# A hybrid decoder layer on one core: both products of a recurrence pair ahead of their copies, attention values in 32-column quarters beside page sets, and longer planner leads

## The chip, the cores and the metric

The kernel runs on one core of a Trainium2 chip. TensorE (PE) multiplies and transposes into PSUM banks; VectorE (DVE), ScalarE (ACT) and GpSimd (POOL) work on SBUF and, DVE and ACT, on PSUM; the queues of SyncE (SP), ACT and POOL start the transfers. The metric is the device time of one launch, in microseconds (us).

## What is computed

One layer for 512 prompt tokens and 8 sequences of 4 sample tokens (TOK = 544 columns). Two branches run in parallel: MoBA attention (block-sparse, over 2048 cached rows of each sample sequence) and an HGRN2 recurrence. They are merged by gates, and a convolutional FFN follows. The recurrence of the reference, cut:

```python
def step(S, xs):
    qc, kc, gc, vc = xs
    b = jnp.cumsum(gc, axis=2)
    diff = jnp.where(tri[...], b[:, :, :, None, :] - b[:, :, None, :, :], -jnp.inf)
    A = jnp.einsum('bhtd,bhsd,bhtsd->bhts', qc, kc, jnp.exp(diff))
    o = jnp.einsum('bhts,bhsv->bhtv', A, vc) + jnp.einsum('bhtd,bhdv->bhtv', qc * jnp.exp(b), S)
    S_new = jnp.exp(b_last)[..., None] * S + jnp.einsum('bhsd,bhsv->bhdv', kc * jnp.exp(b_last - b), vc)
    return S_new, o
...
o_b = rmsnorm(o_b, hg_norm_g) * silu(hg)
y_a = jnp.dot(o_a, w_a_out)
y_b = jnp.dot(o_b, w_b_out)
mixed = sigmoid(ga) * y_a + sigmoid(gb) * y_b
x = x + g1 * jnp.dot(mixed, w_o)
```

## The kernel before

All activations are feature-major: 128 features on the partitions, 544 token columns in two halves of 272. Each large product is split into three of reduced type (`hi*xh + hi*xl + lo*xh`, L123 by way of `gemm_chunk` and `pieces`); ACT makes `whi` and DVE makes `wlo` of each weight tile (L195, L198). Such a product, out `g`, is called a gemm row here. The layer runs in stages: the first projections (to 55 us of the span), then a woven stage, then `w_b`, `w_o`, the FFN.

In the woven stage PE's order is written by a planner at build time. `Paced` keeps a planned time `pe.t` that grows with each product, by 0.095 more when the shape of the array (rows, columns) changes. The main chain is the list of jobs `ORDER` and `LAST` (projections) and then the eight `w_a` jobs. Beside it run `Side` generators: each `yield` names a lead, the planned time after which it wants PE again, and whether it is `tiled` (its products use 32 or 64 of 128 columns). `serve` is asked between gemm chunks (12 gemm rows): it runs the earliest due side; a lone tiled one waits up to `SLACK` for company. When the jobs run out, `finish_sides` runs the remaining sides with nothing between them. The other engines' orders are set by the scheduler, which may run their work early.

The sides are: `moba` (32 page sets: 16 of scores, `ms<-pg`, then 16 of values, `macc<-pg`), `attention` (four head pairs m by four query blocks q: scores, softmax on DVE and ACT, transposes of `K` into `s` banks, values `acc<-eb,vtm`), `recur` (four heads j by eight levels of `LEVELS + (0,)`, taken in four pairs), `ada_rest` (the rest of the modulation, 16 transfers `wadl`, ending in a transpose of `smr`), and `recur_sample` (states of the sample sequences `in_S`, then norms of the outputs `ob`, four statistics `s<-EX,con`).

Of one head's recurrence: `level_ready` makes the operands `EX` of a level; `level_mm` multiplies them, and for the levels from 16 down DVE then copies the wanted entries by mask into `Ab` and `As` (L991, L994). `rec_turn` and `rec_state` make the states, `rec_gather` and `rec_out` the output `ob`. PSUM has eight banks: `g` (3, rotating), `s` (2, rotating), `ms`, `acc`, `macc`.

After the fourth statistic, ACT takes logarithm and exponential of the scales `rr`; DVE multiplies `ob` by `rr` (L198) and by gate and gain (L1232), ACT rounds `obh`, DVE makes `obl`; then the `w_b` products (`g<-obh`) start.

## Time and profile before

| | |
|---|---|
| time before, median of 3 runs | 1011.13 us (1010.74 to 1011.80) |
| the profiled execution's own time | 1011.28 us |
| its span, first to last instruction | 1009.6 us |
| PE busy | 958.6 us, 95% of the span |
| DVE, ACT, POOL busy | 579.6, 474.2, 104.7 us |
| woven stage, in the span | about 55 to 517 us |

PE's busy time counts matmuls that overlap, with modelled ends, so that the distance from one start to the next says more than the duration of one. An idle time with a releaser behind an arrow tells which engine's instruction ended last before the work could go on.

### The profile page before, as it was taken

Reading aid. Unit: us, or ns where it says so; the run is one execution under the profiler, and the core shown is the slowest. Engines: PE = TensorE matmul, PEld = TensorE weight load, DVE = VectorE, ACT = ScalarE, POOL = GpSimd, SP = SyncE. Lnnn points to the kernel's source line nnn. Section 1 sums busy time; section 2 is a strip of 40 time slices with the busy share of each in tenths; the row PEclk is TensorE's granted clock in tenths of the full one; section 3 lists DMA queues with packets and bytes.
Section 4 is the critical chain, followed back from the end, with each engine's and each line's share of the span. In section 5 each row is a group of like instructions: output and inputs, shape, how many; then the busy total and the mean of one; then the engine's idle time right before and its main releaser. Section 6 shows DMA issues by size and latency. Waiting matters only on the chain.

```text
span 1009.6 us, 23648 instructions
## 1 busy us (share of the span) xinstructions
PE 958.6 (95%) x8759; PEld 874.3 (87%) x8759; DVE 579.6 (57%) x1479; ACT 474.2 (47%) x938; POOL 104.7 (10%) x162
## 2 busy tenths in 40 slices
PE   5899999999999989999999999999999999999994
PEld 3898887776778878868998999999999999999994
DVE  4654646644767766435657767655555555555553
ACT  3354565636454633313624556544444444555552
POOL 1212212212210000000013220000000000011111
PEclk9899999999999999999999999999999999999997
DMA  9799999889893555562225514322222223566662
GB/s 313 272 352 345 338 324 319 301 301 317 298 328 139 215 181 171 175 243 94 76 82 200 168 43 138 124 84 93 86 84 93 86 94 93 156 177 170 205 179 71
DMA packets 95894, 190.05 MB, mean 188 GB/s; under 512 B 10657, under 2 KB 26146, under 8 KB 93730
## 3 DMA queue, kind: packets, MB, share of 16 engines
q1 hardware_dynamic: 82722, 141.03, 42.2%
q0 software_dynamic: 8160, 26.75, 7.4%
q10 hardware_dynamic: 4896, 20.76, 5.7%
q8 instruction: 69, 1.13, 0.4%
q14 instruction: 47, 0.39, 0.1%
HBM read 181.47 MB, written 7.02 MB: 187 GB/s over the span
## 4 chain that ended last, share of the span: by engine, by line
PE 82%; DVE 6%; ACT 4%; DMA 3%; issue 2%; POOL 1%; SPq 1%; DVEq 0%; ACTq 0%; POOLq 0%
PE g L123 67%; PE macc L123 4%; PE ms L123 4%; PE s L123 3%; PE acc L123 2%; DMA s<-in_S 1%; PE g L127 1%; PE s L127 1%; DVE wlo L198 1%; ACT whi L195 1%; DMA wadl<-in_w_adl 1%; POOL tgb L1244 1%; DMA xt<-in_x 1%; DMA wraw<-in_w_o 1%; SPq L355 0%
## 5 line engine op out<-in xcount | busy, mean ns | idle before, releaser
L198 DVE TENSOR_TENSOR wlo<-wraw,whi 128x512 fp32r<-128x512 f32 (+1 forms) x300 | 202.4, 676 | 212.0 <-ACT whi L195 208.1
L195 ACT ACTIVATE whi<-wraw 128x512 fp32r<-128x512 f32 (+1 forms) x300 | 185.5, 619 | 274.4 <-PE g L123 256.0
L123 PE MATMUL g<-hh,whi 128*128 128x272 f32 x712 | 213.8, 301 | 2.0 <-ACT hh L195 1.4
L123 PE MATMUL g<-hh,wlo 128*128 128x272 f32 x712 | 206.6, 290 | 0.6 <-DVE wlo L484 0.5
L123 PE MATMUL g<-hl,whi 128*128 128x272 f32 x712 | 206.5, 290 | 0.4 <-DVE hl L1246 0.4
L123 PE MATMUL g<-h2h,whi 128*128 128x272 f32 x704 | 202.4, 289 | 0.0
L123 PE MATMUL g<-h2l,whi 128*128 128x272 f32 x704 | 201.4, 288 | 0.0
L123 PE MATMUL g<-h2h,wlo 128*128 128x272 f32 x704 | 198.9, 288 | 0.0
L123 PEld LDWEIGHTS g<-hh,whi 128*128 128x128 f32 x712 | 135.3, 190 | 17.9 <-issue 11.4
L123 PEld LDWEIGHTS g<-hl,whi 128*128 128x128 f32 x712 | 135.3, 190 | 1.1 <-DVE hl L1246 0.6
L123 PEld LDWEIGHTS g<-hh,wlo 128*128 128x128 f32 x712 | 135.0, 190 | 1.1 <-DVE wlo L484 0.8
L123 PEld LDWEIGHTS g<-h2l,whi 128*128 128x128 f32 x704 | 132.5, 188 | 0.1
L123 PEld LDWEIGHTS g<-h2h,whi 128*128 128x128 f32 x704 | 132.3, 188 | 0.2
L123 PEld LDWEIGHTS g<-h2h,wlo 128*128 128x128 f32 x704 | 130.9, 188 | 0.0
L123 PE MATMUL g<-ah,wlo 128*128 128x272 f32 x352 | 101.4, 288 | 1.2 <-DVE wlo L198 1.2
L123 PE MATMUL g<-ah,whi 128*128 128x272 f32 x352 | 101.8, 289 | 0.0
L123 PE MATMUL g<-al,whi 128*128 128x272 f32 x352 | 101.6, 288 | 0.0
L123 PEld LDWEIGHTS g<-ah,wlo 128*128 128x128 f32 x352 | 66.1, 188 | 1.5 <-DVE wlo L198 1.4
L123 PEld LDWEIGHTS g<-ah,whi 128*128 128x128 f32 x352 | 66.3, 188 | 0.1
L123 PEld LDWEIGHTS g<-al,whi 128*128 128x128 f32 x352 | 66.2, 188 | 0.1
L1286 POOL TENSOR_TENSOR sq<-sq,sq 128x272 f32<-128x272 f32 x24 | 21.3, 886 | 384.8 <-ACT sq L1277 384.7
L1380 DVE SCALAR_TENSOR_TENSOR cv<-U,sv,cv 128x560 f32<-128x560 f32 x44 | 35.3, 802 | 16.5 <-ACT cv L1378 15.7
(317 smaller groups left out, 1484.9 us busy)
## 6 DMA issues: line engine op xcount, KB each, us to landing
wraw<-in_w_up SPq DMA_DIRECT2D x98, 256.0 KB, 2.5
wraw<-in_w_in SPq DMA_DIRECT2D x82, 256.0 KB, 4.5
wraw<-in_w_down SPq DMA_DIRECT2D x80, 256.0 KB, 2.8
pg<-in_K SPq DMA_DIRECT2D x77, 256.0 KB, 6.3
pg<-in_V SPq DMA_DIRECT2D x77, 256.0 KB, 6.3
wadl<-in_w_adl ACTq DMA_DIRECT2D x16, 1024.0 KB, 5.3
pg<-in_K POOLq DMA_DIRECT2D x51, 256.0 KB, 5.9
pg<-in_V POOLq DMA_DIRECT2D x51, 256.0 KB, 6.2
```

The source lines that it names most:

```text
L123: return self.eng.matmul(out, lhsT, rhs, **kw)
L127: return self.eng.transpose(out, in_, ident)
L195: return act.activation(out, in_, AF.Copy, scale=scale)
L198: return dve.tensor_tensor(out, a, b, op=op)
L1244: pool.tensor_tensor(tgb[:, m], tga[:, m], tgb[:, m], op=OP.add)
L1286: pool.tensor_tensor(sqa[f], sqa[f], s, op=OP.add)
L1380: dve.scalar_tensor_tensor(a, U[:, t:t + W], cw[:, t, j:j + 1], a, op0=OP.mult, op1=OP.add)
```

## The change

Seven things change, all in the woven stage.

1. Pairs of levels: `level_mm` loses its copies, which become `level_keep`; `recur` calls both products and then both copies. A result tile `pb` holds two levels and not three, so that each pair has a bank of its own; `big` moves from an `s` bank to `ms`; `rec_turn` and `rec_state` move from `g` banks to `s` banks.
2. Level 64 is computed as 8 products of 32 columns for 4 of 64.
3. Attention values are computed as four products of 32 columns where there were two of 64, and each group is a side of its own (`aside`, tiled, slack 8.0), which is dropped in beside a page set, or run by `values()` before the next transposes at the latest.
4. `pot` and `vst` are padded with zeros to 128 rows (memsets on POOL).
5. Leads: `LV` 6.0 to 7.0, attention's scores to transposes 3.0 to 4.0 (plus 0.8 q), `rec_out` 3.5 to 6.5, `moba_own` 0 to 4.0, the first value set of the second group 0 to 3.0, `smr` 1.5 to 4.0, statistics 2.0 and 1.2 to 3.5 and 1.5.
6. `recur_sample` loads the first two states earlier, waits 5.0 before the transpose of `vi`, and 4.0 where it waited 8.0 for the first pair of states.
7. `Side` has a slack of its own.

```diff
@@ -49,7 +49,7 @@
 WR, WS = 4, 3
-SLACK, LT, SETS, LV, ADA = 2.5, 3.0, 7.2, 6.0, 3.6
+SLACK, LT, SETS, LV, ADA = 2.5, 3.0, 7.2, 7.0, 3.6
 ORDER = "k0 v0 k1 k2 k3 v1 v2 v3 f0 q0 i0 f1 q1 i1 f2 q2 i2 f3 q3 i3 a0 a1 a2 a3 a4 a5 a6 a7 g0 g1 g2 g3"
@@ -131,8 +131,8 @@
-    def __init__(self, gen, due=0.0, tiled=False):
-        self.gen, self.due, self.tiled = gen, due, tiled
+    def __init__(self, gen, due=0.0, tiled=False, slack=None):
+        self.gen, self.due, self.tiled, self.slack = gen, due, tiled, SLACK if slack is None else slack
@@ -276,7 +276,7 @@
                 run(flat[0])
-            elif due and (len(due) > 1 or pe.t - due[0].due > SLACK or pe.mode[1] < 128):
+            elif due and (len(due) > 1 or pe.t - due[0].due > due[0].slack or pe.mode[1] < 128):
                 run(due[0])
@@ -510,7 +510,8 @@
     ks = pM.tile([128, 4, 32], F32, name="ks")
-    vst = pM.tile([32, 512], F32, name="vst")
+    vst = pM.tile([128, 512], F32, name="vst")
+    pool.memset(vst, 0.0)
     qT, kT, vtm, vts, halfway = {}, {}, {}, {}, {}
@@ -654,8 +655,9 @@
         pe.transpose(tb[:32, :128], po_, ident)
-        pot = pM.tile([32, 128], F32, name="pot", tag="pot", bufs=2)
-        dve.tensor_copy(pot, tb[:32, :128])
+        pot = pM.tile([128, 128], F32, name="pot", tag="pot", bufs=2)
+        pool.memset(pot, 0.0)
+        dve.tensor_copy(pot[:32], tb[:32, :128])
         d["rl"], d["pot"] = l9[:, 9:10], pot
@@ -678,10 +680,11 @@
             yield 1.0
+        yield 4.0
         tb = gbank()
             pe.transpose(tb[:32, 128 * m:128 * m + 128], vs[:, m], ident)
-        dve.tensor_copy(vst, tb[:32, :])
+        dve.tensor_copy(vst[:32], tb[:32, :])
@@ -717,6 +720,8 @@
                         yield 1.0
+                    if what is moba_values and g and not j:
+                        yield 3.0, True
                     what(g, j)
@@ -780,9 +785,9 @@
         for j in range(q + 1):
-            for h2 in (1, 0):
-                pe.matmul(acc[64 * h2:64 * h2 + 64, 128 * q:128 * q + 128], vtm[m][:, 128 * j + 64 * h2:128 * j + 64 * h2 + 64],
-                          pTs[h2][:, 128 * j:128 * j + 128], start=j == 0, stop=j == q, skip_group_check=True)
+            for y in (3, 2, 1, 0):
+                pe.matmul(acc[32 * y:32 * y + 32, 128 * q:128 * q + 128], vtm[m][:, 128 * j + 32 * y:128 * j + 32 * y + 32],
+                          pTs[y // 2][:, 128 * j:128 * j + 128], start=j == 0, stop=j == q, skip_group_check=True)
         if q == 3:
@@ -790,33 +795,41 @@
     def attention():
-        past, parts = None, {}
+        parts, past = {}, []
+
+        def values():
+            if past:
+                attend_values(*past.pop())
+
+        def aside():
+            values()
+            return
+            yield
+
         for m in range(4):
...
                 parts[m] = attend_split(m)
-                if past:
-                    yield 2.0, True
-                    attend_values(*past)
-                    past = None
                 yield 5.0
             acc = None
+            if m:
+                yield 2.0
             for q in range(4):
                 ps_ = attend_scores(q, *parts[m])
-                if past:
-                    attend_values(*past)
                 if q == 3 and m + 1 in qT and m + 1 in kT:
                     parts[m + 1] = attend_split(m + 1)
-                yield 3.0 + 0.8 * q
+                yield 4.0 + 0.8 * q
+                values()
                 acc = acc or abank()
...
                     yield 1.0
-                past = (m, q, acc, pTs)
+                past.append((m, q, acc, pTs))
+                sides.append(Side(aside(), pe.t + 1.8 + 0.3 * q, True, 8.0))
                 yield 1.8 + 0.3 * q
         yield 0.5, True
-        attend_values(*past)
+        values()
@@ -911,7 +924,7 @@
     def rec_turn(j, k2):
-        tb = gbank()
+        tb = sbank()
         for c in range(4):
@@ -922,7 +935,7 @@
             return
-        tb = gbank()
+        tb = sbank()
         for c in range(4):
@@ -961,11 +974,12 @@
         if h == 64:
-            big[j] = sbank()
+            big[j] = msbank()
             for c in range(4):
-                a = col(c)
-                pe.matmul(big[j][0:64, 64 * c:64 * c + 64], L[:, a:a + 64], R[:, a + 64:a + 128],
-                          start=True, stop=True, skip_group_check=True)
+                for y in range(2):
+                    a = col(c) + 32 * y
+                    pe.matmul(big[j][32 * y:32 * y + 32, 64 * c:64 * c + 64], L[:, a:a + 32], R[:, col(c) + 64:col(c) + 128],
+                              start=True, stop=True, skip_group_check=True)
             return
@@ -975,22 +989,28 @@
         bi = li - 2
-        if bi % 3 == 0:
+        if bi % 2 == 0:
             pb[j] = sbank()
-        z = 128 * (bi % 3)
+        z = 128 * (bi % 2)
         for c in range(4):
...
         r = slice(32 * j, 32 * j + 32)
-        zs = 384 + 32 * (bi % 3)
+        zs = 256 + 32 * (bi % 2)
         if h <= 2:
                       skip_group_check=True)
+
+    def level_keep(j, li):
+        if li < 2:
+            return
+        bi, r = li - 2, slice(32 * j, 32 * j + 32)
+        z, zs = 128 * (bi % 2), 256 + 32 * (bi % 2)
         dve.copy_predicated(Ab[j], base[:, bi, None, :].to_broadcast([128, 4, 32]),
                             pb[j][:, z:z + 128].rearrange("p (c t) -> p c t", c=4))
-        if h <= 2:
+        if bi > 2:
             dve.copy_predicated(As[r], base[r, bi, :], pb[j][r, zs:zs + 32])
@@ -1001,7 +1021,7 @@
                             big[j][64 * y:64 * y + 32, 256:384].rearrange("p (c t) -> p c t", c=4))
-        later(3.5, lambda: rec_out(j))
+        later(6.5, lambda: rec_out(j))
@@ -1043,6 +1063,8 @@
             level_mm(j, li + 1)
+            level_keep(j, li)
+            level_keep(j, li + 1)
             if li + 2 == n:
@@ -1063,7 +1085,7 @@
         dve.tensor_copy(sm, pa)
-        yield 1.5
+        yield 4.0
         pt = gbank()
@@ -1133,10 +1155,20 @@
+    s0s = {}
+
+    def s0_load(p):
+        s0s.clear()
+        for j in (p, p + 1):
+            s0s[j] = pT_.tile([128, 2 * TOK], F32, name="s0", tag="s0", bufs=2)[:, :1024].rearrange("p (b d) -> p b d", b=8)
+            sync.dma_start(s0s[j], i["S0"][j])
+
     def recur_sample():
...
             yield 1.0
+        s0_load(0)
+        yield 5.0
         tb = gbank()
@@ -1156,14 +1188,14 @@
         for p in range(0, G_H, 2):
-            s0s, rvs = {}, {}
+            rvs = {}
+            if p:
+                s0_load(p)
             for j in (p, p + 1):
...
                    bsel[:96, :, None].to_broadcast([96, NB, 128]), OP.mult)
-                s0s[j] = pT_.tile([128, 2 * TOK], F32, name="s0", tag="s0", bufs=2)[:, :1024].rearrange("p (b d) -> p b d", b=8)
-                sync.dma_start(s0s[j], i["S0"][j])
-            yield 8.0, True
+            yield (8.0 if p else 4.0), True
             for g in range(2):
@@ -1198,7 +1230,7 @@
             sq_ = act.activation(sq, ob[j], AF.Square)
-            yield (2.0 if j == 0 else 1.2)
+            yield (3.5 if j == 0 else 1.5)
             for f in range(2):
```

How the order of PE and DVE moves, at three places. The first is PE at the last pair of head 0 (levels 1 and 0; operands `EX`, and `Q`, `K`). Before:

```order
L123 MATMUL g<-hl,whi 128x272
L123 MATMUL g<-hh,wlo 128x272
L123 MATMUL s<-EX 32x32 [waits DVE_49,Activation_49]
L123 MATMUL s<-EX 32x32 x16
L123 MATMUL s<-Q,K 32x32 [waits DVE_49]
L123 MATMUL s<-Q,K 32x32 x16
```

and after the change:

```order
L123 MATMUL macc<-vst,pot 32x512 x3
L123 MATMUL s<-EX 32x32 [waits DVE_49,Activation_49]
L123 MATMUL s<-EX 32x32 x16
L123 MATMUL s<-Q,K 32x32 x17
L123 MATMUL g<-hh,whi 128x272
L123 MATMUL g<-hl,whi 128x272
```

The second product has lost its wait for DVE. The second place is PE around the last statistic (`s<-EX,con`), ahead of the `w_b` products. Before:

```order
L123 MATMUL g<-hl,whi 128x272
L123 MATMUL g<-hh,wlo 128x272
L123 MATMUL s<-EX,con 128x272 x2
L123 MATMUL g<-hh,whi 128x272
L123 MATMUL g<-hl,whi 128x272
```

and after:

```order
L123 MATMUL g<-oal,whi 128x272
L123 MATMUL g<-oah,wlo 128x272
L123 MATMUL s<-EX,con 128x272 x6
L123 MATMUL g<-obh,whi 128x272 x3
L123 MATMUL g<-obl,whi 128x272
L123 MATMUL g<-obh,wlo 128x272
```

Before, 72 gemm rows of gate jobs and the 192 of `w_a` (`oah`, `oal`) stand between the last statistic and the first `g<-obh`; now none does, and the last three statistics stand together. The third place is DVE, from the last scales `rr<-s` to the last `obl`. Before:

```order
L1205 TENSOR_SCALAR rr<-s 128x272 [waits PE_49]
L198 TENSOR_TENSOR wlo<-wraw,whi 128x512 [waits DMAHW6_49,Activation_49]
L1232 SCALAR_TENSOR_TENSOR ob<-ob,hg_8871,G_7469 128x544 [waits DVE_49]
L1232 SCALAR_TENSOR_TENSOR ob<-ob,hg_8871,G_7618 128x544 [waits DVE_49]
L198 TENSOR_TENSOR wlo<-wraw,whi 128x512 [waits DMAHW7_49,PE_49,Activation_49]
L198 TENSOR_TENSOR ob<-ob,rr 128x544 [waits Activation_49]
L198 TENSOR_TENSOR ob<-ob,rr 128x544 [waits DVE_49]
L198 TENSOR_TENSOR obl<-ob,obh 128x544 [waits Activation_49]
L1232 SCALAR_TENSOR_TENSOR ob<-ob,hg_8871,G_7736 128x544 [waits DVE_49]
L198 TENSOR_TENSOR obl<-ob,obh 128x544 [waits Activation_49]
```

and after:

```order
L1237 TENSOR_SCALAR rr<-s 128x272 [waits PE_49] x3
L198 TENSOR_TENSOR ob<-ob,rr 128x544 [waits DVE_49,Activation_49]
L198 TENSOR_TENSOR ob<-ob,rr 128x544 [waits DVE_49]
L1264 SCALAR_TENSOR_TENSOR ob<-ob,hg_8974,G_7226 128x544 [waits DVE_49]
L1264 SCALAR_TENSOR_TENSOR ob<-ob,hg_8974,G_7480 128x544 [waits DVE_49]
L198 TENSOR_TENSOR ob<-ob,rr 128x544 [waits Activation_49]
L198 TENSOR_TENSOR ob<-ob,rr 128x544
L198 TENSOR_TENSOR obl<-ob,obh 128x544 [waits Activation_49]
L1264 SCALAR_TENSOR_TENSOR ob<-ob,hg_8974,G_7956 128x544 [waits DVE_49]
L198 TENSOR_TENSOR obl<-ob,obh 128x544 [waits Activation_49]
L1264 SCALAR_TENSOR_TENSOR ob<-ob,hg_8974,G_8078 128x544 [waits DVE_49]
L198 TENSOR_TENSOR obl<-ob,obh 128x544 [waits Activation_49] x2
```

All twelve operations on `ob` and `obl` (4 by `rr`, 4 by gate, 4 remainders) now stand behind the last scale, with no split of weights among them.

## Rows read from the trace of the kernel before

**Rows 1.** The page: busy time, share of the span, instructions of each engine.
```profile
PE 958.6 (95%) x8759; PEld 874.3 (87%) x8759; DVE 579.6 (57%) x1479; ACT 474.2 (47%) x938; POOL 104.7 (10%) x162
```

**Rows 2.** PE's waits: total us, times, longest us.
```profile
PE acc L123 <- DMA s<-in_S: 2.0, 1, 2.0
PE g L127 <- DVE smr L1065: 1.8, 1, 1.8
...
PE macc L123 <- DVE S L702: 1.7, 1, 1.7
...
PE g L127 <- DVE vi L848: 1.4, 1, 1.4
```

**Rows 3.** Groups by form: x count | busy us, mean ns | idle before, releasers.
```profile
L123 PE MATMUL acc<-eb,vtm 128*64 128x128 f32 x160 | 12.3, 283 | 0.0
L127 PE MATMUL s<-con,K 128*128 128x128 f32 x80 | 12.0, 275 | 3.2 <-DVE K L766 1.4 <-ACT F L195 0.9 <-ACT whi L195 0.5
L123 PE MATMUL s<-EX 128*32 128x32 f32 x720 | 11.5, 198 | 6.2 <-DVE Ab L991 5.6 <-ACT F L195 0.5
...
L123 PE MATMUL s<-Q,K 128*32 128x32 f32 x136 | 2.0, 199 | 2.3 <-DVE As L994 2.3
```

**Rows 4.** Timeline, PE, at a pair: start, us, line op, count [idle before <-releaser].
```profile
276.24 0.29 PE L123 MATMUL g<-hh,wlo 128*128 128x272 f32 x1
276.46 0.46 PE L123 MATMUL s<-EX 128*32 128x32 f32 x32
277.44 0.46 PE L123 MATMUL s<-EX 128*32 128x32 f32 x32 [0.52 <-ACT F L195]
```

**Rows 5.** Timeline, PE: a group of attention values and the page set behind it.
```profile
120.43 1.09 PE L123 MATMUL acc<-eb,vtm 128*64 128x128 f32 x16
121.45 1.93 PE L123 MATMUL ms<-pg,qbd 128*32 128x256 f32 x32
```

**Rows 6.** Timeline, PE: four transposes into one quarter of the columns.
```profile
154.82 0.61 PE L127 MATMUL g<-con,vs 128*32 128x128 f32 x4
```

**Rows 7.** Timeline, PE: the second pair of sample states, waiting for its load.
```profile
451.57 0.62 PE L123 MATMUL acc<-s,QEs 128*32 128x512 f32 x1 [1.97 <-DMA s<-in_S]
...
454.89 0.43 PE L123 MATMUL g<-hh,whi 128*128 128x272 f32 x1
455.12 0.43 PE L123 MATMUL g<-hl,whi 128*128 128x272 f32 x1
```

**Rows 8.** Stretches: us, busy (count) of PE, PEld, DVE, ACT, POOL; PEclk, DMA share, GB/s.
```profile
600.00:900.00 300.00, 300.00 (x2394) 299.87 (x2393) 171.77 (x453) 152.71 (x276) 4.63 (x5) 1.00 0.34 108
452.90:456.30 3.40, 3.40 (x11) 2.24 (x10) 1.60 (x7) 0.00 (x0) 0.00 (x0) 0.50 0.01 3
```

**Rows 9.** Timeline, PE: the last statistic, and the first product of `w_b`.
```profile
482.39 1.08 PE L123 MATMUL s<-EX,con 128*128 128x272 f32 x4
...
517.11 0.29 PE L123 MATMUL g<-obh,whi 128*128 128x272 f32 x1
```

**Rows 10.** Timeline, ACT, behind the last square: table load, logarithm.
```profile
478.72 0.66 ACT L1200 ACTIVATE EX<-ob 128x544 f32<-128x544 f32 x1 [0.18 <-PE s L123]
479.39 1.28 ACT L1207 ACT_TABLE_LOAD   x1
480.69 1.11 ACT L1209 ACTIVATE rr<-rr 128x1088 f32<-128x1088 f32 x1
```

**Rows 11.** Timeline, DVE: scales, gates and last remainder of the outputs.
```profile
483.40 1.35 DVE L198 TENSOR_TENSOR ob<-ob,rr 128x544 f32<-128x544 f32 x2
...
485.62 1.48 DVE L1232 SCALAR_TENSOR_TENSOR ob<-ob,hg,G 128x544 f32<-128x544 f32 x2
...
497.24 0.72 DVE L198 TENSOR_TENSOR obl<-ob,obh 128x544 fp32r<-128x544 f32 x1
```

**Rows 12.** Timeline, DVE and PE: the last operand of another pair, and that pair.
```profile
351.45 0.42 DVE L198 TENSOR_TENSOR EX<-EX,Q 128x256 f32<-128x256 f32 x1
...
353.08 0.48 PE L123 MATMUL s<-EX 128*32 128x32 f32 x32
```

## Prediction

> **What bounds the kernel now.** I read the page first: PE is busy 95% of the span and the next engine 57% [rows 1], so the question is where PE stands still or works for nothing, and not how fast the others are. The list of PE's waits comes next [rows 2], then idle time by kind of product [rows 3], then the timeline at the places that both name. All the waits that this change can reach lie in the woven stage. Outside it PE is dense: 2394 products in 300 us of the FFN, 0.1253 us each, at the full granted clock [rows 8]. I use 0.125 for a gemm row below.
>
> **Part by part: the pairs of levels.** In a pair PE runs the 16 or 17 products of one level, waits until DVE has copied them, and runs the next level [rows 4]. There are 16 pairs; four are levels 64 and 32, which have no copy between them, so 12 pauses remain. The idle time named by form is 6.2 + 2.3 = 8.5 us [rows 3]. It counts from the modelled end of the last product; products start about 0.01 us apart when nothing holds them (32 rows in 0.46, one row alone lasting 0.198 [rows 3, 4]), so each pause also costs the 0.19 us in which a row drains: 12 x 0.19 = 2.3. Together 10.8. The pair shown bears it out: 0.98 us from start to start, of which 16 products need 0.26. After the change the second product stands ahead of both copies, in a bank that only its own pair uses, and nothing is late next as long as its operand is there. The closest case of the 12 is a pair that began at 353.08 with its last operand finished at 351.87 [rows 12], 1.2 us earlier, and the lead to it grows. I take -10.3, between -5.5 (half the pauses return as waits for operands) and -10.8.
>
> **Changes of array width.** From a gemm row to a 32-column product the step is 0.22 us where 0.125 is usual [rows 4]; a switch costs 0.095. Walking through both orders product by product I count 144 switches before and 122 after: quarters share the width of the page sets, level 64 that of level 32, and the padded `vst` and `pot` that of their set. 22 x 0.095 = -2.1.
>
> **Quarters.** A step is two products (4 rows) on two halves of the array; the 40 steps are 160 rows [rows 3]. Four steps (16 rows) take 1.02 us to the next set [rows 5], so a step 0.23 with the switch. In four strips the same 128 columns pass side by side: 0 us, if the four run together as the four of a page set do (32 rows of 256 columns in 1.93 us [rows 5]: 0.06 a row, although one alone would take twice the 0.11 that 128 columns need). If they ran one after another, as four transposes into one strip do (0.11 apart, (0.61 - 0.28) / 3 [rows 6]), a step would take 8 x 0.11 = 0.88, and 40 steps +26. I take 0, since the page set is nearest.
>
> Of the Trainium skill, TensorE: Matmul & The Clock Gate, section "Wait — 56ns, not 53.3ns?", speaks against doubling the count of products: it gives a floor of about 25 ns between starts, and some 62 ns per matmul with hardware decoding off. By 62 ns a step of 8 rows would take 0.5 and the 40 steps +11 us. The level products do not show either floor: 32 rows lie in 0.46 us, so that the trace disagrees and I leave it at 0.
>
> **Other waits that leads reach.** The transpose of `vi` (1.4), of `smr` (1.8), the first value set of the second group (1.7), and the load of the second pair of states (2.0 [rows 2]). The last one is larger in fact: to the 1.97 idle comes the drain of the row before, 0.6, the time that one of this form lasts [rows 7], so 2.55; and the granted clock then was 0.50 for 3.4 us, the lower of its levels, 1.2 GHz [rows 8], with rows 0.23 apart [rows 7], which cost about 1.5 more. Leads grow by 2.5 to 5 us at each, and the loads of `wadl` that shared the queues with `in_S` now lie earlier. Bounds: 0 and 1.6 + 2.0 + 1.75 + 2.55 + 1.5 = 9.4 (each wait with its drain). I take -8.9. Transposes of `K` idle 3.2, 4.1 with the drains [rows 3]; the lead grows by 1 us, but the distance in products at q = 3, where most of it falls, hardly grows: -2.0, bounds 0 and -4.1. Against that, in the changed order one group of values (second head pair, q = 1) stands directly behind its transposes, and PE must wait for two ACT copies: +1.0, bounds 0 and +1.5. The two memsets of `pot` stand early in POOL's order, ahead of the page loads that could hold them, so nobody waits for them: 0.
>
> **The cover ahead of `w_b`.** This is the price. Before, the last statistic starts at 482.39 and the first `w_b` product at 517.11 [rows 9]; between them lie 264 gemm rows, 33 us, under which ACT and DVE finish `ob`. Longer leads push the recurrence and its tail back while the jobs run on; in the changed order none of these rows is left and the last three statistics stand together. So the chain is bare. With t = 0 at the second statistic's start (0.9 us each): its end frees a square buffer, the last square ends at 1.8 (0.66), table load 1.28, then logarithm, exponential, logarithm, exponential of 1.11 each [rows 10]: first exponential at 5.35, second at 7.6. DVE starts at 5.4 and has twelve operations, 0.68 for a scale, 0.74 for a gate, 0.72 for a remainder [rows 11]: four until 8.3, the other eight until 14.0. PE has finished the statistics at 3.3, 0.6 later than dense since each waits for a bank. Until 14.1 it finds 27 rows whose operands are ready (3.4 us; three groups are interleaved). Idle: 14.1 - 3.3 - 3.4 + 0.6 = 8.0. After a pause of this kind the clock fell before [rows 7, 8], so I add 2.0 (the 1.5 us seen there, to 3.0 if it lasts twice as long). Together +10.0, bounds +5 and +13. What hid this was gemm rows; nothing else can.
>
> **Sum.** -10.3 - 2.1 - 8.9 - 2.0 + 1.0 + 10.0 + 1.0 (small new waits that a new order brings; bounds -1 and +4) = -11.3. The profiled execution took 1011.28, 1.7 more than its span; the median is 1011.13, so the two agree. 1011.28 - 11.3 = 1000.0.
>
> **Rivals.** *The tail is hidden after all*: if scales and gates go by quicker, or the rows between fill the hole, it costs 2 for 10: 992.0. For it: the scheduler spread three groups into it. Against: the twelve DVE operations alone last 8.6 us. Chance 0.09.
>
> *Waits move and do not go*: the pairs wait for the second operand instead of the copy, and leads are eaten because the planner's time and real time part. Half the gains (23.3 / 2) remain against +12: 1011.6, within 0.2% of the time before. For it: the margin of only 1.2 us [rows 12]. Against: that pair's lead grows, and it is the closest. Chance 0.10.
>
> *The clock stays low behind the hole* (slower side): PE comes out of the hole with scattered rows, and if the clock then stays at 1.2 GHz through the 192 rows of `w_b`, each costs 0.23 - 0.125 = 0.10 more, +20 for the 2 in the sum: 1018. It decides from some 133 rows on ((11.3 + 2) / 0.10). For it: the hole is longer than the wait at 449 us. Against: there the clock was back after 3.4 us of work. Chance 0.04.
>
> *Quarters run one after another* (slower too): +26, 1026. Against it are the page sets. Chance 0.02.
>
> **How the numbers follow.** My forecast, 1000.0, has 0.75: with the ends that I hold plausible it reaches from 993 to 1007. The range takes in part of the two nearest rivals: 992 to 1009. 0.2% is 2.0 us and about what a measurement of this kernel can tell from no change, so faster means under 1009.1: forecast and hidden tail, with a third of the moved waits, 0.87; same 0.06; slower 0.07.
>
> **What would show it.** Right: in the changed profile the waits on `Ab` and `As` are gone from PE's list; the waits on `vi`, `smr`, `in_S` and `S` are gone; a new one stands at the first `obh` and `obl`, 6 to 10 us in sum, around 495 us, with the granted clock at half just behind it; value groups show 32 columns and the same 0.2 us per step. Wrong: PE waits inside pairs for `EX`; or the hole is under 4 us; or PE waits for pages, whose transfers share queues that carry more per us when PE is faster.

## The result and the profile after

The changed kernel takes 999.43 us (median of 4 runs, 998.9 to 1001.82) against 1010.93 (median of 4 runs of the kernel before beside them): a ratio of 0.9894, 95% interval 0.9872 to 0.9916. That is 11.5 us faster; the prediction said 11.3 and 1000.0 us. The profiled execution took 999.2 us; its span is 997.5, 12.1 less than before, and the times read from traces below are of these two spans.

The page of the changed kernel, busy time of each engine, answers to [rows 1]:

```profile
PE 954.1 (96%) x8951; PEld 875.8 (88%) x8951; DVE 577.5 (58%) x1479; ACT 474.4 (48%) x939; POOL 104.4 (10%) x165
```

PE has 192 products more (160 of values, 32 of level 64) and is busy 4.5 us less. Its list of waits (total us, times, longest us) answers to [rows 2]:

```profile
PE g L123 <- ACT obh L195: 4.1, 1, 4.1
PE s L127 <- DVE K L771: 2.4, 4, 0.9
...
PE g L123 <- ACT tga L1100: 1.3, 1, 1.3
...
PE g L123 <- DVE obl L198: 0.9, 1, 0.9
PE macc L123 <- DMA wadl<-in_w_adl: 0.8, 1, 0.8
...
PE acc L123 <- ACT eb L195: 0.6, 1, 0.6
```

The four waits of [rows 2] (`in_S`, `smr`, `S`, `vi`) are gone, and no wait on `Ab` or `As` is left. New are the first `obh` and `obl` of `w_b`, a bank of a gate job that ACT empties late (`tga`), one transfer `wadl` and the values directly behind their transposes (`eb`). The groups by form answer to [rows 3]:

```profile
L127 PE MATMUL s<-con,K 128*128 128x128 f32 x80 | 12.3, 277 | 3.0 <-DVE K L771 2.4 <-ACT K L769 0.3
...
L123 PE MATMUL acc<-eb,vtm 128*32 128x128 f32 x320 | 12.0, 276 | 0.6 <-ACT eb L195 0.6
L123 PE MATMUL s<-EX 128*32 128x32 f32 x656 | 8.5, 198 | 0.0
...
L123 PE MATMUL s<-Q,K 128*32 128x32 f32 x136 | 2.2, 198 | 0.0
```

Idle time before the levels fell from 6.2 + 2.3 to 0, that before the transposes of `K` hardly (3.2 to 3.0). A pair in PE's timeline, which answers to [rows 4]:

```profile
287.25 0.76 PE L123 MATMUL s<-EX 128*32 128x32 f32 x64
287.84 1.50 PE L123 MATMUL macc<-pg,pT 128*32 128x512 f32 x12
```

Both levels (64 rows) now go by in 0.59 us, where the pair shown before needed 1.27. The price stands at the end of the woven stage, PE's timeline from the last statistics on (it answers to [rows 9]):

```profile
491.89 1.08 PE L123 MATMUL s<-EX,con 128*128 128x272 f32 x4
493.14 0.70 PE L123 MATMUL s<-EX,con 128*128 128x272 f32 x2 [0.17 <-DVE rr L1237]
493.99 1.99 PE L123 MATMUL s<-EX,con 128*128 128x272 f32 x6 [0.16 <-DVE rr L1237]
500.12 1.05 PE L123 MATMUL g<-obh,whi 128*128 128x272 f32 x3 [4.14 <-ACT obh L195]
502.03 0.59 PE L123 MATMUL g<-obl,whi 128*128 128x272 f32 x1 [0.87 <-DVE obl L198]
```

Between them lies the chain that the prediction laid out: on ACT and DVE the last exponential, the first product with the scales and the last remainders (they answer to [rows 10] and [rows 11]):

```profile
498.32 1.11 ACT L1243 ACTIVATE rr<-rr 128x1088 f32<-128x1088 f32 x1
```

```profile
497.32 1.36 DVE L198 TENSOR_TENSOR ob<-ob,rr 128x544 f32<-128x544 f32 x2 [0.86 <-ACT rr L1243]
...
503.92 1.53 DVE L198 TENSOR_TENSOR obl<-ob,obh 128x544 fp32r<-128x544 f32 x2
```

Two stretches of that place (busy time and count of PE, PEld, DVE, ACT, POOL; granted clock, DMA share, GB/s) answer to [rows 8]:

```profile
497.80:508.10 10.30, 7.11 (x30) 6.80 (x31) 7.56 (x12) 4.21 (x6) 0.00 (x0) 0.50 0.00 0
508.10:528.70 20.60, 20.57 (x164) 20.35 (x164) 17.30 (x26) 7.83 (x13) 10.62 (x7) 1.00 0.42 131
```

The granted clock fell to 0.50 (1.2 GHz) while PE stood idle and came back at 508.1. To see where the 12.1 us lie, I added up for each kind of product the time from its start to the start of the next one, from 60 us to the first product of `w_b`:

| | before | after | |
|---|---|---|---|
| products of levels | 23.1 | 11.7 | -11.4 |
| sample states (`s,QEs`, `rv,k2x`) | 9.7 | 5.7 | -4.0 |
| attention values | 12.9 | 9.9 | -3.0 |
| statistics, to the first `w_b` product | 2.9 | 8.9 | +6.1 |
| all PE products | 457.1 | 440.1 | -17.0 |

Of the values' 3.0, some 1.75 is the wait on `S`, which before the change stood behind the last group of values; the rest is the change of width, below. `w_b` itself then takes 28.5 us from first to last product where it took 24.0, which gives 4.5 back; behind it the two kernels differ by 0.3 us.

### The profile page after: what moved, and what is told of

It is laid out like the page before. It is cut to its first block, busy times and chain, and to the rows that moved or that the text cites. A ratio compares the mean times of both kernels' runs of the same rounds, so it can differ in the third digit from the quotient of the medians.

```text
span 997.5 us, 24024 instructions
## 1 busy us (share of the span) xinstructions
PE 954.1 (96%) x8951; PEld 875.8 (88%) x8951; DVE 577.5 (58%) x1479; ACT 474.4 (48%) x939; POOL 104.4 (10%) x165
## 4 chain that ended last, share of the span: by engine, by line
PE 85%; DVE 5%; ACT 4%; DMA 2%; issue 2%; SPq 1%; POOL 0%; DVEq 0%; ACTq 0%; POOLq 0%
PE g L123 70%; PE macc L123 4%; PE ms L123 4%; PE s L123 3%; PE acc L123 2%; PE s L127 1%; PE g L127 1%; DVE wlo L198 1%; DMA wadl<-in_w_adl 1%; DMA xt<-in_x 1%; DMA wraw<-in_w_o 1%; SPq L355 0%; ACT hh L398 0%; DVE hsr L198 0%; ACT tga L650 0%
## 5 line engine op out<-in xcount | busy, mean ns | idle before, releaser
L1412 DVE SCALAR_TENSOR_TENSOR cv<-U,sv,cv 128x560 f32<-128x560 f32 x44 | 35.3, 802 | 16.5 <-ACT cv L1410 15.8
```

The costliest lines, as they stand in the source:

```text
L1412: dve.scalar_tensor_tensor(a, U[:, t:t + W], cw[:, t, j:j + 1], a, op0=OP.mult, op1=OP.add)
```

## Experiments

The question was not whether the sum was right but whether its terms were. Each run is compared with the changed kernel (999.4) or the kernel before (medians of 1010.3 to 1011.3 in the several sets of runs).

### The pairs alone

In the kernel before, only the first edit is made: both products, then both copies, each pair's result in a bank of its own.

```diff
             level_mm(j, li)
             level_mm(j, li + 1)
+            level_keep(j, li)
+            level_keep(j, li + 1)
```

> The kernel before with the first edit alone: both products of a pair ahead of their copies, each pair's result in a bank of its own, and level 64 in the ms bank; the leads, the values in halves and the order of PE's products are those of before, and the 264 gemm rows of cover ahead of w_b stay. Theory (the pairs are worth what the prediction gave, 10.3 us): the waits on Ab and As leave PE's list and the time falls by 10.3, from 1010.9 to about 1000.6 (998.5 to 1002). Rival (waits move and do not go): PE waits for EX or for DVE inside the pairs instead, at most half is left, so 1005.5 or more.

Measured: 1006.09 us (5 runs), ratio 0.9955 (0.9935 to 0.9975), a gain of 4.9, so that the number falls to the rival, but not for its reason. PE's order is that of before, save a few neighbouring products that start almost together, so the two traces can be laid over each other. For the products of levels the time from each start to the next falls from 23.1 us to 12.3, by 10.9; no wait for `EX` appears. The waits are elsewhere:

```profile
PE acc L123 <- DVE hs L1008: 4.7, 2, 2.6
...
PE g L127 <- DVE smr L1073: 1.8, 1, 1.8
```

`hs` at L1008 is the last copy of `rec_gather`, which the first product of `rec_out` needs. PE's timeline and DVE's at the first of the two places, head 0:

```profile
300.42 0.71 PE L123 MATMUL acc<-hs,V 128*128 128x128 f32 x4 [2.08 <-DVE hs L1008]
```

```profile
297.01 0.42 DVE L198 TENSOR_TENSOR EX<-EX,K 128x256 f32<-128x256 f32 x1 [0.84 <-ACT EX L955]
...
298.98 0.56 DVE L886 TENSOR_SCALAR F<-F,lb 128x544 f32<-128x544 f32 x1 [1.21 <-ACT F L884]
299.45 0.41 DVE L1006 COPY hs<-ms 64x256 f32<-64x256 f32 x1
299.79 0.57 DVE L1008 COPY hs<-ms 32x128 f32<-32x128 f32 x2
```

DVE at the same place in the kernel before:

```profile
298.78 0.57 DVE L1002 COPY hs<-s 32x128 f32<-32x128 f32 x2
299.38 0.56 DVE L886 TENSOR_SCALAR F<-F,lb 128x544 f32<-128x544 f32 x1
```

PE comes 1.8 us earlier to this point and stands 2.3 us longer there. The copies of the gather stand in DVE's order behind operations that wait for ACT (0.84 and 1.21 idle); the second of these, `F` at L886, stood behind them before, so that they now end at 300.36 where they ended at 299.35. At head 1 the same costs 2.75; heads 2 and 3 do not wait. So 5.0 of 10.9 us are handed back at the next consumer of the same chain.

That the rest comes near the measured gain is chance, for three more things differ. Behind the wait at head 1 the granted clock stood at 0.50 from 344.0 to 347.4, which cost 1.7 us, and the half clock at the start of `w_o` (last section) some 1.6. Against these, the wait on `in_S` is gone with the half clock behind it, 3.5 us, although no lead of the loads was changed.

### The pairs and the lead of `rec_out`

To the edit above the lead of `rec_out` is added.

```diff
-        later(3.5, lambda: rec_out(j))
+        later(6.5, lambda: rec_out(j))
```

> The kernel before with the pairs edit and the lead of rec_out at 6.5 for 3.5, nothing else; 168 gemm rows of cover stay ahead of w_b. The run of the pairs edit alone gained 10.6 us in the pairs and gave 5.0 back at two places, the first product of rec_out of heads 0 and 1, which waited for the copies that now stand later in DVE's order. Theory (that wait is all that took the gain, and the longer lead covers it): the two waits on hs are gone and the time is some 5 below that run's 1006.1, about 1001. Rival (the wait is not covered by 3 us of lead, or moves on to the next step of the chain): 1004 or more, with hs, ob or a DMA in PE's list by 3 us or more.

Measured: 995.78 us (4 runs), 0.9862 (0.9847 to 0.9878): 10.3 us less than the pairs alone, twice what the theory asked for. The two waits on `hs` are gone, as expected. The rest I did not expect: the wait on `smr` (2.0 with its drain) is gone too, although its lead is the old one, and so are the two stretches at half clock that the pairs alone had, behind head 1 (1.7) and at the start of `w_o` (1.6). Another 0.7 lies ahead of the first page set, where neither edit acts. What stays of the old waits:

```profile
PE macc L123 <- DVE S L702: 1.7, 1, 1.7
PE g L127 <- DVE vi L848: 1.5, 1, 1.5
```

These two edits give more than the whole change, because 168 gemm rows stay ahead of `w_b` and nothing is lost there.

### The copies between the products again

The other side: in the changed kernel each copy goes back between the two products.

```diff
             level_mm(j, li)
-            level_mm(j, li + 1)
             level_keep(j, li)
+            level_mm(j, li + 1)
             level_keep(j, li + 1)
```

> The changed kernel with the copies of a level again between the two products of its pair, in the bank that only the pair uses; the order of PE's products is that of the changed kernel. Theory (the pairs' gain comes from the copies alone): the waits on Ab and As are back with about 0.98 us from product to product in 12 pairs, and the time rises by 10, from 999.4 to about 1009.7. Rival (the pairs gained by longer leads and the new banks, not by the copies): less than +5. Rival (the chain of outputs, not PE, sets the end of the woven stage, so what PE loses in the pairs is slack there): +6 or less, the hole ahead of w_b shrinking by the rest.

Measured: 1006.57 us (7 runs), 0.995 (0.9934 to 0.9965), 7.1 above the changed kernel. Waits of PE:

```profile
PE s L123 <- DVE Ab L1011: 3.5, 7, 0.6
PE s L123 <- DVE As L1014: 2.7, 4, 0.8
```

The list names eleven pauses (7 + 4); by the starts all twelve are back. Product by product the second levels come 0.62 to 1.00 us later each, 8.8 in sum; for the products of levels the time to the next start rises from 11.7 to 20.5. The hole ahead of `w_b` stays (4.1 on `obh`), so what PE loses in the pairs is no slack there. Between them PE wins back 2.8 at waits that its slowness covers (`tga` 1.5, `wadl` 0.67, a gemm row 0.66) and 1.0 in `w_b`, and loses 1.7 at a half clock at the start of `w_o` and 0.6 in the first 26 us of the span. Both rivals fall, and the theory holds in kind: a pause is worth 0.73 us and not the 0.83 that 10 us would need, and the time shows less than twelve of them, since each microsecond also shifts other waits.

### A shorter lead for the levels: cover back ahead of `w_b`

```diff
-SLACK, LT, SETS, LV, ADA = 2.5, 3.0, 7.2, 7.0, 3.6
+SLACK, LT, SETS, LV, ADA = 2.5, 3.0, 7.2, 6.0, 3.6
```

> The changed kernel with LV at 6.0 for 7.0 and nothing else: the recurrence ends earlier in the order, and 108 gemm rows (13.5 us) stand between the last statistic and the first product of w_b, where none did. Theory (the hole ahead of w_b costs about 9.5 us: 4.3 idle, 0.65 at the statistics, about 4.5 inside w_b at half clock and in waits): all of that goes, against at most 3 us of new waits for EX; 999.4 falls to 990 to 993. Rival (the shorter lead brings the waits into the pairs, for EX): 996 or more, with EX in PE's list by 4 us or more. Rival (the gaps only move to another place, because the time is set by DVE or by pages): 998 to 1000.

Measured: 992.0 us (4 runs), 0.9797 (0.977 to 0.9824), 7.4 under the changed kernel, and the fastest of all. The stretch from the last statistic to `w_b`, and `w_b`:

```profile
483.80:497.50 13.70, 13.70 (x110) 13.66 (x109) 13.70 (x27) 6.96 (x11) 0.00 (x0) 1.00 0.23 78
497.58:521.60 24.02, 24.02 (x194) 24.02 (x193) 17.47 (x30) 8.57 (x14) 11.03 (x7) 1.00 0.46 135
```

The hole is closed: the statistics are back at 2.9 us for 8.9, and `w_b` takes 23.9 for 28.5. That is 6.1 + 4.6 = 10.7 us; the pairs did not begin to wait for `EX`. The profiled execution (993.35 us) is 5.9 under that of the changed kernel, and what lies between went to the new order and to chance: 3.6 ahead of `w_b` (2.0 at gemm rows, of which 0.6 because the stage begins 0.6 later and the rest mostly a half clock from 311.0 to 314.4, and 1.0 behind `g<-con,S`) and 1.3 at a half clock at the start of `w_o`. The median ends inside the range that the theory gave.

### The hole filled with work

In the changed kernel 32 gemm rows are added behind the last statistic; their result is not used.

```diff
     finish_sides(su, al_, rec)
+    fb = mbank()
+    for _ in range(32):
+        pe.matmul(fb[:, :HALF], oah[:, 0, 0:128], oah[:, 1, half(0)], start=True, stop=True)
```

> The changed kernel with 32 gemm rows whose result nobody uses behind the last statistic, some 4.0 us of work in the hole of 4.3. Theory (after the hole the granted clock is low for 10 us and that is what makes w_b 4.5 us longer): with the hole filled the granted clock stays at 1.00 (rows 0.125 apart from the first w_b row on, save where they wait for the last remainder), and the time falls by 2 to 4 us, to about 996.5. Rival (w_b is longer because its first groups wait for the last obh and obl, whatever the clock): within 1 us of 999.4. A third way (the clock falls all the same, in the short waits behind): within 1 us too, with the clock at 0.50 in the rows behind the filler.

Measured: 996.77 us (4 runs), 0.9849 (0.9825 to 0.9874); this interval just touches that of the changed kernel, so the verdict rests on the trace. PE's timeline, and the two stretches of the hole and of `w_b`:

```profile
495.88 4.42 PE L123 MATMUL macc<-oah 128*128 128x272 f32 x32
500.40 0.64 PE L123 MATMUL g<-obh,whi 128*128 128x272 f32 x3
502.30 0.39 PE L123 MATMUL g<-obl,whi 128*128 128x272 f32 x1 [1.26 <-DVE obl L198]
```

```profile
496.00:500.30 4.30, 4.30 (x34) 4.03 (x32) 3.15 (x6) 4.24 (x5) 0.00 (x0) 1.00 0.00 1
500.30:526.75 26.45, 25.06 (x192) 24.31 (x193) 22.73 (x35) 9.85 (x17) 10.59 (x7) 1.00 0.34 103
```

The first `w_b` product starts as late as before (500.40 for 500.12), since its operand decides, but the granted clock stays at 1.00 and `w_b` takes 26.3 us for 28.5. So the half clock behind the hole costs 2.2 us, and the waits for remainders inside `w_b` the other 2.3 (26.3 - 24.0). In the changed kernel the two lie partly over each other: 26 rows of `w_b` start 0.227 us apart there, 2.6 more than at 0.125, while the last remainder is not ready before 505.45 in any case. Both the theory and its first rival hold a half.

### Values in halves again

```diff
-            for y in (3, 2, 1, 0):
-                pe.matmul(acc[32 * y:32 * y + 32, 128 * q:128 * q + 128], vtm[m][:, 128 * j + 32 * y:128 * j + 32 * y + 32],
-                          pTs[y // 2][:, 128 * j:128 * j + 128], start=j == 0, stop=j == q, skip_group_check=True)
+            for h2 in (1, 0):
+                pe.matmul(acc[64 * h2:64 * h2 + 64, 128 * q:128 * q + 128], vtm[m][:, 128 * j + 64 * h2:128 * j + 64 * h2 + 64],
+                          pTs[h2][:, 128 * j:128 * j + 128], start=j == 0, stop=j == q, skip_group_check=True)
```

> The changed kernel with the attention values in halves again: two products of 64 columns for four of 32, each group at the same place of PE's order; the planner then counts 137 switches of array width for 122. Theory (quarters cost nothing in themselves and save the switches, 0.095 each): +1.4 us, about 1000.8, with the value groups of 16 steps as long as before. Rival (quarters cost more than halves, for each has twice the starts, by the floor of 62 ns per product +11 for all 40 steps): the time falls by 5 or more. Rival (a value group costs the same and a switch nothing): within 0.3 of 999.4.

Measured: 1002.6 us (5 runs), 0.9919 (0.9905 to 0.9933), 3.2 above the changed kernel, with intervals that overlap. The values by form:

```profile
L123 PE MATMUL acc<-eb,vtm 128*64 128x128 f32 x160 | 12.3, 283 | 0.6 <-ACT eb L195 0.6
```

The time from each value product to the next start is 11.15 us in halves and 9.87 in quarters, 1.28 less. Inside the groups quarters need 7.64 and halves 7.91: in both, the strips start together (0.004 to 0.018 us apart) and the next set of strips some 0.1 behind, so that four strips pass in the time of two. The price of a switch shows at the edges of the groups: ahead of page products the last product of a group takes 0.20 us to the next start in halves and 0.09 in quarters (9 groups), and behind page products a group starts 0.11 us later in halves (5 groups). That is 0.11 a switch for the 0.095 used; the entries, some 0.6 in all, are not in the 1.28. The profiled execution is 4.7 us longer than that of the changed kernel: 3.0 of that lie at the start of `w_o` (a wait of 1.2 and a half clock of 17 rows) and 0.9 ahead of the first page set, both far from the values. So the theory holds by the trace, where the times alone would not settle it; the floor of 62 ns a product does not show.

### Four leads undone in the changed kernel

```diff
-        yield 4.0
+        yield 1.5
         pt = gbank()
...
-                    if what is moba_values and g and not j:
-                        yield 3.0, True
...
-        s0_load(0)
-        yield 5.0
...
-            yield (8.0 if p else 4.0), True
+            yield 8.0, True
```

(The loads of the states stand at their old place again.)

> The changed kernel with four leads as before: the transpose of smr (1.5), the first value set of the second group (none), the transpose of vi (none) and the loads of the sample states at their old place, with 8.0 ahead of the first pair. In its order 33 gemm rows (4.1 us) stand ahead of w_b, none in the changed kernel. Theory (these four leads are worth what the prediction gave): the waits on smr (1.8), vi (1.4), S (1.7) and in_S (2.0) are back at their sizes, and up to the first statistic PE loses 7.9 to 9.4 us; the hole ahead of w_b then shrinks by about 4, so that the time comes to 1003.5 to 1005. Rival (the waits left because of the new order, not because of the leads): fewer than two of the four are back, and the time is 995 to 999.

Measured: 995.39 us (4 runs), 0.9846 (0.983 to 0.9861): not slower, but 4.0 faster than the changed kernel. In PE's list only one of the four waits is back:

```profile
PE g L127 <- DVE vi L859: 1.5, 1, 1.5
```

`smr`, `S` and `in_S` stay away without their leads; the transfers of `in_S`, which took up to 9.9 us from issue to landing before, take at most 4.9 here (but up to 11.0 with the pairs and the lead of `rec_out` alone, where PE does not wait for them either). The theory falls, the rival holds. The time falls because 33 gemm rows come to stand in the hole: its first `w_b` product starts 3.8 us earlier, counted from the first page set.

### The same four leads alone in the kernel before

The edit is the one above the other way round, in the kernel before.

```diff
-        yield 1.5
+        yield 4.0
         pt = gbank()
...
+                    if what is moba_values and g and not j:
+                        yield 3.0, True
...
+        s0_load(0)
+        yield 5.0
...
-            yield 8.0, True
+            yield (8.0 if p else 4.0), True
```

> The kernel before with four leads alone, the other side of the run that undid them in the changed kernel: smr 4.0 for 1.5, the first value set of the second group 3.0 for none, the loads of the sample states earlier, 5.0 ahead of the transpose of vi, and 4.0 for 8.0 at the first pair of states. Pairs, LV and all else are as before; cover ahead of w_b stays (329 gemm rows). Theory (in the order of before the leads are what removes the waits on smr 1.8, S 1.7, vi 1.4 and in_S 2.0 with its drain and half clock): all four are gone and the time falls by 7.9 to 9.4, to about 1002. Rival (waits of this kind come and go with the order and return elsewhere): two or more of the four stay, or others of 3 us or more appear, and the time is 1005 or more.

Measured: 1017.02 us (5 runs), 1.0056 (1.0031 to 1.0081): slower by 5.8. PE's waits:

```profile
PE s L123 <- DVE Ab L993: 4.9, 8, 1.0
PE g L123 <- DVE oas L709: 3.5, 1, 3.5
PE s L123 <- DVE As L996: 3.1, 4, 1.4
...
PE acc L123 <- DVE hs L1004: 2.5, 1, 2.5
PE g L127 <- ACT tgb L1080: 2.0, 1, 2.0
PE acc L123 <- DMA s<-in_S: 1.7, 1, 1.7
```

`vi` and `S` are gone, 3.1 us. `smr` has left the list by name only: the transpose that it feeds waits 2.0 us (1.8 before), now for its bank, which ACT empties behind a table load and a scale:

```profile
487.26 0.66 PE L127 MATMUL g<-con,smr 128*128 128x128 f32 x4 [2.00 <-ACT tgb L1080]
```

`in_S` stays, and `oas` (3.5) and `hs` (2.5) are new; behind each of these two the granted clock stood at 0.50 (260.7 to 264.1, 346.0 to 349.4). Waits came and went with the order, as the rival said. Of the 5.7 us by which the profiled execution is longer, 1.7 lie ahead of the first page set, where no lead acts.

### A longer lead for the transposes of `K`

```diff
-                yield 4.0 + 0.8 * q
+                yield 6.0 + 0.8 * q
```

> The changed kernel with 6.0 for 4.0 in the lead from attention's scores to their transposes. The prediction gave the transposes of K a gain of 2.0 that did not come: PE still waits 2.4 for K in the changed kernel, and its groups of transposes start to start are 0.3 longer than before. Theory (the lead is still too short): the waits on K fall below 0.8 and the time falls by 1.5 to 3, to about 997, with the hole ahead of w_b as it is. Rival (K's copies come late because of what stands ahead of them on DVE and ACT, or the waits move to the values behind the transposes): waits on K and eb of 2 or more in sum, the time within 1.5 of 999.4.

Measured: 1015.97 us (9 runs), 1.0048 (1.0031 to 1.0065), 16.5 above the changed kernel: neither expectation. The waits on `K` are gone and the transposes take 4.4 us less (the gaps ahead of and inside their groups, 9.7 for 14.1), as the theory said. But PE's list now has:

```profile
PE acc L123 <- DMA s<-in_S: 6.3, 2, 4.5
...
PE g L123 <- ACT obh L195: 4.6, 1, 4.6
PE acc L123 <- DVE osum L1220: 4.5, 1, 4.5
```

Attention now ends at 289.8 for 263.9, and with it all sides behind it move; between the last `rec_out` and the last statistic stand 120 gemm rows for 348, and from 465 to 517 us PE works on 169 products in 52 us. The chain of the sample states has lost its cover, as the chain of `ob` had in the changed kernel.

## Why the prediction came true, term by term

**Pairs, -10.3: right, with a condition that the text lacked.** The pauses were worth 10.9 us (the pairs alone) and 8.8 (the way back), though the time showed 4.9 and 7.1. "Nothing is late next as long as its operand is there" looked only at the second product. What is late next is `rec_out`, whose copies lie on DVE behind work that waits for ACT: 5.0 us, seen with the pairs alone. The longer lead of `rec_out`, which the prediction named nowhere as a condition, took it away when it was added to the pairs; the changed kernel has that lead, and no wait on `hs`.

**Switches -2.1, quarters 0: right.** A switch measured 0.11 for 0.095 on 14 of the 22, and quarters cost nothing in their groups; the seven switches of level 64 and of the padded operands were not measured by themselves. The Trainium skill, TensorE: Matmul & The Clock Gate, section "Wait — 56ns, not 53.3ns?", gives a floor of about 25 ns between starts, and 62 ns per matmul with hardware decoding off. Neither shows here: quarters start 7.64 / 304 = 0.025 us apart, but only as a mean of 240 gaps under 0.02 us and 64 of about 0.09, and 64 level rows lie in 0.59 us.

**Other leads, -8.9: the sum right, the reason wrong.** In the changed kernel all four waits are gone: sample states -4.0 (2.55 + 1.5 had been taken; the 2.55 held 0.4 that such a row needs without a wait), the gap ahead of `smr` from 2.10 to 0.13, ahead of `vi` from 1.69 to 0.52, and the wait on `S` has left the list. But undone there, only `vi` returned, and alone they cost 5.8 us. Run by run: `vi` belongs to its lead, gone with the leads alone and back without them. `in_S` was gone with the pairs alone and stayed with the leads alone. `smr` went when the lead of `rec_out` joined the pairs, and with the leads alone its transpose waited as long for its bank. `S` went with the leads alone, but stayed away without them in the changed order; which of the other edits does that is not settled. A lead moves one side and with it the rest of the planner's order, and the size of this term came out right in part by luck.

**Transposes of `K`, -2.0: wrong.** The gaps ahead of and inside the groups are 13.5 us before and 14.1 after. Idle time ahead of them is 3.0 for 3.2 [rows 3], 2.4 of it on `K` by DVE and 0.3 by ACT, and the gaps do not shrink. The text saw itself that the distance in products hardly grew, and yet took half; the lead of 6.0 showed that the waits can go, for a price at the other end of the stage.

**Values behind their transposes, +1.0: right,** 0.7 (0.90 from start to start where 0.20 is usual).

**Cover ahead of `w_b`, +10.0: right in sum and in parts.** The statistics up to the first `w_b` product cost 6.1 more and waits inside `w_b` 2.3: 8.4 for the 8.0 of idle time; the half clock cost 2.2 for 2.0. Both together are 10.6, and the version with cover recovered 10.7. The list's two waits sum to 5.0 (4.1 on `obh`, 0.9 on `obl`), under the 6 to 10 named as a sign: the last statistic ended 4.1 us after the second one's start and not 3.3, so that the hole began later. The chain of ACT and DVE ran as laid out: from the second statistic's start at 491.89 the first exponential ends after 5.4 us (5.35 had been given), the second after 7.5 (7.6) and the last remainder, at 505.45, after 13.6 (14.0).

**Small new waits, +1.0: too low and too high.** `tga` cost 1.5 and `wadl` 0.9. Against them, gaps that nobody had counted are gone: 0.8 behind the transposes of `vs`, 0.5 at `pot`.

So four terms were right as they were worked out (pairs, switches, values, cover) and one in size but not in cause (leads). The transposes of `K` were taken 2.5 too well, and gaps that nobody had counted and small surpluses of other terms made up for it: that the sum came within 0.2 us of the measured gain is luck. Of the rivals, "waits move and do not go" is what happens to the pairs without the lead of `rec_out` (995.8 with it, 1006.1 without), and to the leads in the order of before. That the clock stays low through `w_b` did not come: it was back after 8.0 us of `w_b`.

## What to carry to other kernels

An operation taken off PE's path by letting it run behind the next product can make somebody else wait: follow its result to the next consumer on PE, and ask what stands ahead of it in the copying engine's order. Where a planner weaves chains into a supply of independent rows, those rows are a store that can be spent once; before lengthening a lead, count how many are left beside each chain behind it (264 before, 0 after, 108 in the fastest version). A wait in PE's list belongs to the whole order: before a lead is given the credit for removing it, add the lead alone and take it away alone.

## What was not expected of the hardware

The granted clock can fall at waits of the same length in one kernel and not in another. At the start of `w_o` PE waits 1.4 us for `woh` in all kernels here; 14 to 17 rows 0.227 us apart followed in the pairs alone (548.0 to 552.0), with the copies between, with values in halves and with `LV` at 6.0, and in none of the seven others, the kernel before and the changed kernel among them. From the pairs alone, PE's timeline:

```profile
547.99 0.39 PE L123 MATMUL g<-hh,woh 128*128 128x272 f32 x1 [1.44 <-ACT woh L195]
548.22 0.28 PE L123 MATMUL g<-hl,woh 128*128 128x272 f32 x1
548.72 0.58 PE L123 MATMUL g<-hh,wol 128*128 128x272 f32 x1 [0.21 <-DVE wol L198]
```

It costs 1.3 to 1.7 us, so that differences between versions of that size can't be put down to an edit without a look at this place. What decides it stays open. With `LV` at 6.0 the clock also fell at 311.0, to 0.50 until 314.4, in the second of two idle times of only 0.55 and 0.74 us with eight rows of 16 columns (`g<-con,S`) between them; behind the waits of 1.8 on `smr` and 1.7 on `S` in the kernel before it did not fall. After the hole of 4.1 us the clock was low from 497.8 to 508.1, 10.3 us, of which 2.3 fell into the idle time.
